# Scattering expert outputs with ScalarE and GpSimd instead of VectorE, with seven split-weight buffers and seven loaded tiles instead of five and nine

## The chip, the cores and the metric

The kernel runs on one core of a Trainium2 chip. The metric is the device time of one launch in microseconds (us). The core has five engines that each work through their own list of instructions in order and wait for each other through semaphores: TensorE (PE in the profile; its weight loads are PEld), VectorE (DVE), ScalarE (ACT), GpSimd (POOL) and SyncE (SP), which here issues the large loads from memory.

## What is computed

A trunk of two layers over 256 latent and 256 context tokens of width 1024. Each layer has a token mixer and a channel mixer. In the second layer the channel mixer is a mixture of experts, and only the latent tokens go through it:

```
def swiglu(u, w1, w3, w2):
    return (jax.nn.silu(u @ w1) * (u @ w3)) @ w2

def moe_swiglu(u, router_w, router_b, w1, w3, w2):
    logits = (u @ router_w + router_b).astype(F32)
    top_v, top_i = lax.top_k(logits, TOP_K)            # 2 of 8 experts
    gates = jax.nn.softmax(top_v, axis=-1)
    combine = jnp.sum(jax.nn.one_hot(top_i, N_EXPERTS, dtype=F32) * gates[..., None], axis=-2)
    out = jnp.zeros_like(u)
    for e in range(N_EXPERTS):                         # w1, w3: 1024 x 2816, w2: 2816 x 1024
        out = out + combine[..., e:e + 1] * swiglu(u, w1[e], w3[e], w2[e])
    return out
...
h_lat = layer_norm(ALPHA * h_lat + mod_l[5] * f_lat, ln_g, ln_b)
```

## The kernel before

All matrices are float32. A product is made of three passes of the faster fp32r type: each operand is cast to fp32r (its high part), the difference to the original is its low part, and `mm3` adds high times high, high times low and low times high (lines 107 to 109). For a weight this is the work of `split`: 1024 columns of a loaded tile are cast by ScalarE into `whi` (L126), and VectorE subtracts to get `wlo` (L127). One such pair is called a split below; six matmuls of 512 columns use it. Five pairs of buffers (the pool `wp`) hold the splits that wait for TensorE or are in use, so ScalarE can be at most five ahead.

The mixture is run in units of up to 128 tokens for one expert; `moe` has seven units written out, and a loop behind them for further ones, which does not run on this input. For each unit, `gather` picks the rows with a one-hot matmul, `turn` transposes them, `up` makes one of six chunks of 512 hidden columns (w1 and w3; the last has 256), `turn_g` transposes the result, `down` multiplies by w2 into the two accumulators `Y`, and after the sixth chunk `scatter` brings `Y` back to the rows of the tokens. Work of the next unit is interleaved with the end of one: its first `up` chunk stands ahead of the last `down`, and its second `up` chunk runs beside the scatter. Weights come as tiles of 1 MB (`wtile`), issued by SyncE in the order of use into nine buffers: seven of the pool `rawb` and two of `rawp`. A tile makes two splits and is free for the next load when VectorE has read it for the second `wlo`.

`scatter` first splits `Y` into `yh` (ScalarE) and `yl` (VectorE). For each of four quarters (two groups of 128 tokens, two halves of 512 columns) TensorE makes a one-hot matmul into a bank of the tag `T`, of which there are two; VectorE takes it out of PSUM, scaling it by the combine weight `cu` of each row and by the modulation `gate` of each column (L1131), into a tile `sct`; and GpSimd adds it to the residual stream `hl` (L1132). `sct` comes from the pool `mo`, which holds two buffers of each name. The last unit passes `quick=True` and does part of its adds on VectorE.

The order of each engine's list is fixed when the program is built, by a scheduler that sees all dependences; nothing is reordered on the chip. An instruction that waits holds up all that stand behind it on its engine.

Of the kernel before, what the change touches and what calls it, by code (L numbers as in the profile page):

```python
# [15 lines left out]
F32 = mybir.dt.float32  # L16
# [3 lines left out]
AF = mybir.ActivationFunctionType  # L20
ALU = mybir.AluOpType
# [3 lines left out]
P = 128  # L25
# [51 lines left out]
class Trunk:  # L77
# [41 lines left out]
    def split(self, v, pool=None):  # L119

        nc = self.nc
        a, b = v.shape[1], v.shape[2]
        pool = pool or self.wp
        hi = pool.tile([P, 1024], F32R, name="whi", tag="whi")[:, 0:a * b].rearrange("p (a b) -> p a b", a=a)
        lo = pool.tile([P, 1024], F32R, name="wlo", tag="wlo")[:, 0:a * b].rearrange("p (a b) -> p a b", a=a)
        nc.scalar.copy(out=hi, in_=v)  # L126
        self.last = nc.vector.tensor_tensor(out=lo, in0=v, in1=hi, op=ALU.subtract)  # L127
        return hi, lo
# [988 lines left out]
    def scatter(self, Y, selT, cu, gate, hl, quick=False):  # L1117

        nc, mp = self.nc, self.mp
        yh, yl = (mp.tile([P, D], F32R, name=name, tag="rows") for name in ("yh", "yl"))  # L1120
        for nn in range(2):
            cs = slice(nn * 512, nn * 512 + 512)
            self.split2(yh[:, cs], yl[:, cs], Y[nn])
        for b in range(2):
            for nn in range(2):
                cs = slice(nn * 512, nn * 512 + 512)
                o = self.bank("h" if quick else "T")
                nc.tensor.matmul(o, lhsT=selT[:, b], rhs=yh[:, cs], start=True, stop=False)
                nc.tensor.matmul(o, lhsT=selT[:, b], rhs=yl[:, cs], start=False, stop=True)
                t = mp.tile([P, 512], F32, name="sct", tag="g" if quick and nn else "sct")  # L1130
                nc.vector.scalar_tensor_tensor(out=t, in0=o, scalar=cu[:, b:b + 1], in1=gate[:, cs], op0=ALU.mult, op1=ALU.mult)  # L1131
                (nc.vector if quick and nn else nc.gpsimd).tensor_tensor(out=hl[:, b, cs], in0=hl[:, b, cs], in1=t, op=ALU.add)  # L1132

    def moe_consts(self, ro):

# [107 lines left out]
    def run(self):  # L1243
        tc, nc, i = self.tc, self.nc, self.i
# [4 lines left out]
        with ExitStack() as es:  # L1249
            pool = lambda name, bufs, **kw: es.enter_context(tc.tile_pool(name=name, bufs=bufs, **kw))  # L1250
            self.cp = pool("cp", 1)
            self.stp = pool("stp", 4)
            self.rawp = pool("rawp", 2)
            self.wp = pool("wp", 5)
            pool("edge", 1, side="right").tile([P, 24], F32, name="edge")
            mx = ExitStack()
            right = lambda name, bufs, **kw: mx.enter_context(tc.tile_pool(name=name, bufs=bufs, side="right", **kw))
# [31 lines left out]
            hl = pool("hl", 1).tile([P, 2, D], F32, name="hl")  # L1289
            with tc.tile_pool(name="hc", bufs=1) as hcp:  # L1290
                hc = hcp.tile([P, 2, D], F32, name="hc")
                h = lambda tb: hc[:, tb] if tb < 2 else hl[:, tb - 2]
                with tc.tile_pool(name="raw2", bufs=2) as raw2, tc.tile_pool(name="ga", bufs=1) as gp, tc.tile_pool(name="res", bufs=1) as self.resp:
                    nc.gpsimd.dma_start(out=hc, in_=i["ctx"].rearrange("o (b p) d -> p (o b) d", p=P))
                    nc.gpsimd.dma_start(out=hl, in_=i["x"].rearrange("o (b p) d -> p (o b) d", p=P))
                    gate = self.gate(0, 2, [0, 1], gp)
# [33 lines left out]
            self.moe_consts(pool("rc", 1))  # L1330
            mh, ml = self.mixer(1, uh, ul, lat, bd, self.lru_products(1, uh, ul, True), prepare)
            self.dumpm(mh, ml, 1)
            self.RB, self.wn = 7, 0
            self.rawb = pool("rawb", self.RB)
            ro = pool("ro", 1)
            gate2 = self.gate(1, 5, [0], ro)[0]
            with ExitStack() as ms:
# [54 lines left out]
```

## Time and profile before

| | |
|---|---|
| median of 3 runs | 1671.74 us (1671.57 to 1671.98) |
| the profiled execution | 1673.18 us |
| its span, first to last instruction | 1671.3 us |
| busy share of the span | PE 95%, DVE 73%, ACT 55%, POOL 10% |
| experts' part with the scatters | from about 943 to 1658 us of the span |

The span is that of the one execution that was traced; 1.9 us of its time lie outside it. A matmul's record lasts longer than the distance to the next one, since matmuls overlap in the array, so a busy share of TensorE close to 100% does not say that it runs at its peak, and gaps in its records understate a wait a little.

### The profile page before, as it was taken

Reading aid. Unit: us, or ns where it says so; the run is one execution under the profiler, and the core shown is the slowest. Engines: PE = TensorE matmul, PEld = TensorE weight load, DVE = VectorE, ACT = ScalarE, POOL = GpSimd, SP = SyncE. Lnnn points to the kernel's source line nnn. Section 1 sums busy time; section 2 is a strip of 40 time slices with the busy share of each in tenths; the row PEclk is TensorE's granted clock in tenths of the full one; section 3 lists DMA queues with packets and bytes.
Section 4 is the critical chain, followed back from the end, with each engine's and each line's share of the span. In section 5 each row is a group of like instructions: output and inputs, shape, how many; then the busy total and the mean of one; then the engine's idle time right before and its main releaser. Section 6 shows DMA issues by size and latency. Waiting matters only on the chain. (4 is left out here: it accounts for less than half of the span.)

```text
span 1671.3 us, 21565 instructions
## 1 busy us (share of the span) xinstructions
PE 1587.6 (95%) x7977; PEld 1229.7 (74%) x7977; DVE 1221.2 (73%) x1741; ACT 919.8 (55%) x1298; POOL 160.9 (10%) x131
## 2 busy tenths in 40 slices
PE   7999999999999999989899799999999999999995
PEld 3776566787777777777567588787887878878784
DVE  2678675644443345687976998989888898888987
ACT  2466565423222223246665487777776776767773
POOL 0000012250000000260002200101001010010101
PEclk8999999999999999989999799999999999999998
DMA  8313446224542354212348599898998989989890
GB/s 304 121 54 104 152 152 201 101 94 158 170 157 101 126 166 162 76 54 82 113 141 285 177 393 358 322 377 304 352 347 312 344 316 341 356 310 335 325 355 31
DMA packets 164582, 364.77 MB, mean 218 GB/s; under 512 B 8396, under 2 KB 46120, under 8 KB 159352
## 3 DMA queue, kind: packets, MB, share of 16 engines
q1 hardware_dynamic: 159472, 355.56, 60.6%
q0 software_dynamic: 1840, 6.67, 1.2%
q10 hardware_dynamic: 3160, 1.12, 0.3%
q8 instruction: 64, 1.05, 0.3%
q14 instruction: 46, 0.38, 0.1%
HBM read 362.27 MB, written 1.05 MB: 217 GB/s over the span
## 5 line engine op out<-in xcount | busy, mean ns | idle before, releaser
L127 DVE TENSOR_TENSOR wlo<-rawb,whi 128x1024 fp32r<-128x1024 f32 x362 | 436.0, 1249 | 34.5 <-ACT whi L126 30.6
L126 ACT CAST whi<-rawb 128x1024 fp32r<-128x1024 f32 x362 | 364.3, 1051 | 57.0 <-PE ps_h L109 33.6
L127 DVE TENSOR_TENSOR wlo<-raw,whi 128x1024 fp32r<-128x1024 f32 x214 | 269.2, 1279 | 100.1 <-ACT whi L126 98.7
L126 ACT CAST whi<-raw 128x1024 fp32r<-128x1024 f32 x214 | 218.7, 1051 | 183.8 <-DMA raw<-in_ffn_w_dram 85.6
L108 PE MATMUL ps_h<-wlo,th 128*128 128x512 f32 (+1 forms) x672 | 257.6, 383 | 14.2 <-DVE wlo L127 13.3
L107 PE MATMUL ps_h<-whi,th 128*128 128x512 f32 (+1 forms) x672 | 253.7, 378 | 0.2 <-ACT th L131 0.2
L109 PE MATMUL ps_h<-whi,tl 128*128 128x512 f32 (+1 forms) x672 | 251.8, 375 | 0.0
L108 PEld LDWEIGHTS ps_h<-wlo,th 128*128 128x128 f32 x672 | 127.3, 189 | 51.2 <-DVE wlo L127 30.6
L107 PEld LDWEIGHTS ps_h<-whi,th 128*128 128x128 f32 x672 | 127.5, 190 | 23.0 <-ACT th L131 0.5
L109 PEld LDWEIGHTS ps_h<-whi,tl 128*128 128x128 f32 x672 | 127.4, 190 | 20.6 <-DVE tl L132 0.2
L108 PE MATMUL ps_Y<-wlo,gTh 128*128 128x512 f32 x308 | 122.4, 397 | 0.4
L109 PE MATMUL ps_Y<-whi,gTl 128*128 128x512 f32 x308 | 120.2, 390 | 0.0
L1132 POOL TENSOR_TENSOR hl<-hl,sct 128x512 f32<-128x512 f32 x26 | 45.0, 1759 | 679.5 <-DVE sct L1131 559.5
L107 PE MATMUL ps_Y<-whi,gTh 128*128 128x512 f32 x308 | 108.4, 390 | 0.0
L107 PE MATMUL ps_acc<-uh,whi 128*128 128x512 f32 (+1 forms) x256 | 92.4, 367 | 2.6 <-ACT whi L126 2.3
L108 PE MATMUL ps_acc<-ul,whi 128*128 128x512 f32 (+1 forms) x256 | 94.1, 368 | 0.1
L109 PE MATMUL ps_acc<-uh,wlo 128*128 128x512 f32 (+1 forms) x256 | 92.1, 361 | 0.0
L108 PE MATMUL ps_S<-ul,whi 128*128 128x512 f32 (+1 forms) x240 | 85.7, 357 | 0.0
L107 PE MATMUL ps_S<-uh,whi 128*128 128x512 f32 (+1 forms) x240 | 85.6, 357 | 0.0
L109 PE MATMUL ps_S<-uh,wlo 128*128 128x512 f32 (+1 forms) x240 | 84.9, 355 | 0.0
L107 PE MATMUL ps_acc<-whi,uh 128*128 128x512 f32 (+1 forms) x176 | 71.0, 403 | 0.0
L108 PE MATMUL ps_acc<-wlo,uh 128*128 128x512 f32 (+1 forms) x176 | 69.1, 392 | 0.2 <-DVE wlo L127 0.2
(352 smaller groups left out, 2830.3 us busy)
## 6 DMA issues: line engine op xcount, KB each, us to landing
rawb<-in_moe_w_dram SPq DMA_DIRECT2D x181, 1024.0 KB, 6.7
raw<-in_moe_w_dram SPq DMA_DIRECT2D x50, 1024.0 KB, 6.5
raw<-in_ada_w_dram SPq DMA_DIRECT2D x40, 1024.0 KB, 4.9
raw<-in_ffn_w_dram SPq DMA_DIRECT2D x33, 1024.0 KB, 7.2
raw<-in_w_in_dram SPq DMA_DIRECT2D x16, 1024.0 KB, 5.6
aw<-in_ada_w_dram SPq DMA_DIRECT2D x16, 512.0 KB, 7.0
raw<-in_w_out_dram SPq DMA_DIRECT2D x16, 512.0 KB, 5.6
lg<-in_ln_g_dram POOLq DMA_DIRECT2D x4, 512.0 KB, 4.0
```

What stands on the lines that cost most here:

```text
L107: mm(out, lhsT=ah, rhs=bh, start=start, stop=False)
L108: mm(out, lhsT=ah, rhs=bl, start=False, stop=False)
L109: mm(out, lhsT=al, rhs=bh, start=False, stop=stop)
L126: nc.scalar.copy(out=hi, in_=v)
L127: self.last = nc.vector.tensor_tensor(out=lo, in0=v, in1=hi, op=ALU.subtract)
L1132: (nc.vector if quick and nn else nc.gpsimd).tensor_tensor(out=hl[:, b, cs], in0=hl[:, b, cs], in1=t, op=ALU.add)
```

## The change

Three edits. In `scatter`, for all units but the last (`quick`), the copy out of PSUM moves from VectorE to ScalarE, which scales by `cu` only; GpSimd multiplies by `gate` and then adds, two instructions where it had one. The split pairs get seven buffers from the start of the second layer's output projection on: the five of `wp` and two of a new pool `wpx`, used in turn. The pool `rawb` shrinks from seven tiles of 1 MB to five, so that seven are loaded ahead instead of nine; the memory that this frees holds `wpx`. A small tile (`shift`) moves the addresses behind it by 384 bytes per partition.

```diff
@@ split
-        pool = pool or self.wp
+        if pool is None:
+            pool = self.wps[self.ws % len(self.wps)]
+            self.ws += 1
@@ scatter
-                nc.vector.scalar_tensor_tensor(out=t, in0=o, scalar=cu[:, b:b + 1], in1=gate[:, cs], op0=ALU.mult, op1=ALU.mult)
-                (nc.vector if quick and nn else nc.gpsimd).tensor_tensor(out=hl[:, b, cs], in0=hl[:, b, cs], in1=t, op=ALU.add)
+                if quick:
+                    nc.vector.scalar_tensor_tensor(out=t, in0=o, scalar=cu[:, b:b + 1], in1=gate[:, cs], op0=ALU.mult, op1=ALU.mult)
+                    (nc.vector if nn else nc.gpsimd).tensor_tensor(out=hl[:, b, cs], in0=hl[:, b, cs], in1=t, op=ALU.add)
+                else:
+                    nc.scalar.activation(out=t, in_=o, func=AF.Copy, scale=cu[:, b:b + 1])
+                    nc.gpsimd.tensor_tensor(out=t, in0=t, in1=gate[:, cs], op=ALU.mult)
+                    nc.gpsimd.tensor_tensor(out=hl[:, b, cs], in0=hl[:, b, cs], in1=t, op=ALU.add)
@@ run
-            self.wp = pool("wp", 5)
+            self.wps, self.ws = [pool("wp", 5)] * 5, 0
...
-            self.RB, self.wn = 7, 0
+            self.RB, self.wn = 5, 0
             self.rawb = pool("rawb", self.RB)
+            pool("shift", 1).tile([P, 96], F32, name="shift")
+            self.wps, self.ws = self.wps + [pool("wpx", 2)] * 2, 0
```

The lists of the engines change with it. On ScalarE, around the scatter of the third unit (`yh` is the split of `Y`, `whi` a cast of weights, `gTh` and `g` belong to `turn_g` and `up`), this stood before:

```order
L126 CAST whi<-rawb 128x1024 x6
L131 CAST yh<-ps_Y 128x512 x2
L126 CAST whi<-rawb 128x1024 x4
L131 CAST gTh<-ps_T 128x512
L126 CAST whi<-raw 128x1024 x2
L1041 ACTIVATE g<-ps_h 128x512
L126 CAST whi<-raw 128x1024 x2
L126 CAST whi<-rawb 128x1024 x8
```

And this stands there now:

```order
L128 CAST whi<-rawb 128x1024 x4
L128 CAST whi<-raw 128x1024 x2
L133 CAST yh<-ps_Y 128x512 x2
L128 CAST whi<-raw 128x1024 x2
L1137 ACTIVATE sct<-ps_T,cu 128x512 x2
L128 CAST whi<-rawb 128x1024
L1137 ACTIVATE sct<-ps_T,cu 128x512 x2
L128 CAST whi<-rawb 128x1024
L1043 ACTIVATE g<-ps_h 128x512
L133 CAST gTh<-ps_T 128x512
L128 CAST whi<-rawb 128x1024 x8
```

The four copies stand in two pairs with one cast of weights between them; the fourth cast after `yh` has moved behind the second pair.

On VectorE, at the same scatter (`wlo` is the low part of a split, `yl` that of `Y`), before:

```order
L127 TENSOR_TENSOR wlo<-rawb,whi 128x1024 x3
L132 TENSOR_TENSOR yl<-ps_Y,yh 128x512 x2
L1131 SCALAR_TENSOR_TENSOR sct<-ps_T,cu,gate_7558 128x512 x2
L127 TENSOR_TENSOR wlo<-rawb,whi 128x1024
L1131 SCALAR_TENSOR_TENSOR sct<-ps_T,cu,gate_7558 128x512 x2
L127 TENSOR_TENSOR wlo<-rawb,whi 128x1024 x2
L132 TENSOR_TENSOR gTl<-ps_T,gTh 128x512
```

Now:

```order
L129 TENSOR_TENSOR wlo<-rawb,whi 128x1024
L129 TENSOR_TENSOR wlo<-raw,whi 128x1024 x2
L134 TENSOR_TENSOR yl<-ps_Y,yh 128x512 x2
L129 TENSOR_TENSOR wlo<-raw,whi 128x1024 x2
L129 TENSOR_TENSOR wlo<-rawb,whi 128x1024 x2
L134 TENSOR_TENSOR gTl<-ps_T,gTh 128x512
```

The four copies are gone from it, and four low parts follow `yl` directly.

## Rows read from the trace of the kernel before

**Rows 1.** The page, part 1: busy us, share of the span, instructions.
```profile
PE 1587.6 (95%) x7977; PEld 1229.7 (74%) x7977; DVE 1221.2 (73%) x1741; ACT 919.8 (55%) x1298; POOL 160.9 (10%) x131
```

**Rows 2.** Windows with a scatter: PE, PEld, DVE, ACT, POOL busy; PEclk; DMA share; GB/s.
```profile
1050.00:1100.00 50.00, 49.32 (x222) 39.86 (x222) 48.20 (x46) 38.30 (x41) 7.03 (x4) 1.00 0.91 339
...
1150.00:1200.00 50.00, 48.48 (x216) 38.85 (x216) 43.36 (x42) 35.92 (x40) 7.02 (x4) 1.00 0.88 317
...
1250.00:1300.00 50.00, 47.18 (x203) 37.59 (x202) 42.60 (x41) 33.07 (x39) 7.02 (x4) 0.97 0.90 319
...
1350.00:1400.00 50.00, 47.03 (x207) 36.92 (x206) 44.23 (x43) 32.83 (x38) 7.02 (x4) 1.00 0.92 327
...
1450.00:1500.00 50.00, 47.09 (x200) 36.90 (x199) 43.50 (x42) 34.73 (x40) 7.01 (x4) 0.97 0.88 316
...
1550.00:1600.00 50.00, 47.00 (x206) 36.70 (x205) 43.98 (x42) 32.93 (x38) 7.01 (x4) 1.00 0.92 334
```

**Rows 3.** Waits, 1040 to 1660 us: total us, times, longest.
```profile
ACT whi L126 <- PE ps_h L109: 30.3, 61, 1.7
...
PE ps_h L108 <- DVE wlo L127: 13.3, 15, 1.2
```

**Rows 4.** Timeline of the third scatter, all engines: start, us, engine, instruction [idle <-releaser].
```profile
1249.70 1.08 ACT L131 CAST yh<-ps_Y 128x512 fp32r<-128x512 f32 x2 [2.07 <-PE ps_Y L109]
...
1249.97 0.40 PE L107 MATMUL ps_h<-whi,th 128*128 128x512 f32 x1
...
1250.20 0.40 PE L108 MATMUL ps_h<-wlo,th 128*128 128x512 f32 x1
...
1250.67 3.90 ACT L126 CAST whi<-rawb 128x1024 fp32r<-128x1024 f32 x4
...
1251.07 1.28 DVE L132 TENSOR_TENSOR yl<-ps_Y,yh 128x512 fp32r<-128x512 f32 x2
...
1252.56 1.44 DVE L1131 SCALAR_TENSOR_TENSOR sct<-ps_T,cu,gate 128x512 f32<-128x512 f32 x2 [0.21 <-PE ps_T L1129]
...
1253.39 7.02 POOL L1132 TENSOR_TENSOR hl<-hl,sct 128x512 f32<-128x512 f32 x4 [94.76 <-DVE sct L1131]
...
1253.91 1.87 DVE L127 TENSOR_TENSOR wlo<-rawb,whi 128x1024 fp32r<-128x1024 f32 x1
...
1255.84 0.50 PE L108 MATMUL ps_h<-wlo,th 128*128 128x512 f32 x1 [0.83 <-DVE wlo L127]
...
1257.32 0.60 PE L1052 MATMUL ps_T<-cst,g 128*128 128x128 f32 x4
...
1257.62 3.87 DVE L127 TENSOR_TENSOR wlo<-rawb,whi 128x1024 fp32r<-128x1024 f32 x2
...
1257.67 0.48 PE L107 MATMUL ps_h<-whi,th 128*128 128x512 f32 x1
...
1259.32 0.50 PE L108 MATMUL ps_h<-wlo,th 128*128 128x512 f32 x1 [1.16 <-DVE wlo L127]
...
1261.55 0.69 PE L108 MATMUL ps_h<-wlo,th 128*128 128x512 f32 x1 [0.82 <-DVE wlo L127]
...
1262.47 0.63 PE L107 MATMUL ps_h<-whi,th 128*128 128x512 f32 x1
```

**Rows 5.** Low parts (`wlo`), 1270 to 1340 us, no GpSimd work: ns min/median/max.
```profile
L127 DVE TENSOR_TENSOR wlo<-rawb,whi x39: 1207/1219/1226, 1269.3 to 1339.0; 128x1024 fp32r<-128x1024 f32 x39
```

**Rows 6.** Tile `sct`, third scatter: ns min/median/max.
```profile
L1131 DVE SCALAR_TENSOR_TENSOR sct<-ps_T,cu,gate x4: 740/750/751, 1252.6 to 1257.0; 128x512 f32<-128x512 f32 x4
L1132 POOL TENSOR_TENSOR hl<-hl,sct x4: 1285/1780/2271, 1253.4 to 1258.1; 128x512 f32<-128x512 f32 x4
```

**Rows 7.** Tile `p` near 885 us, ScalarE from PSUM with one per-row operand: ns min/median/max.
```profile
L614 ACT ACTIVATE p<-ps_S,nb x3: 671/683/688, 880.5 to 886.2; 128x512 f32<-128x512 f32 x3
```

**Rows 8.** SyncE's own waits, 1040 to 1660 us.
```profile
SPq L1006 <- DVE wlo L127: 452.6, 179, 7.5
```

**Rows 9.** The page, part 6: KB each, us from issue to landing.
```profile
rawb<-in_moe_w_dram SPq DMA_DIRECT2D x181, 1024.0 KB, 6.7
```

## The prediction

> **What bounds the kernel now.** I read the page's busy shares first, then the windows, then the waits of the experts' part, then the timeline of one scatter. TensorE is busy 95% of the span [rows 1], so time is won or lost almost only where TensorE stands still. In the windows with a scatter it is busy 49.3, 48.5, 47.2, 47.0, 47.1 and 47.0 of 50 us [rows 2]; that is 0.68 + 1.52 + 2.82 + 2.97 + 2.91 + 3.00 = 13.9 us idle at the six scatters that the change touches. Nearly all of it is one wait: TensorE for the low part `wlo`, 13.3 us in 15 waits [rows 3]. Elsewhere ScalarE waits for TensorE (30.3 us in 61 waits [rows 3]): the five pairs of split buffers are full, and TensorE sets the pace.
>
> Records of matmuls last 0.40 us and start 0.23 us apart [rows 4], so a gap understates a wait by about 0.17 us; 15 waits make 2.4 us, and the loss at the six scatters is about 13.9 + 2.4 = 16.3 us.
>
> The timeline shows who is late. At the third scatter TensorE waits for `wlo` at 1255.84, 1259.32 and 1261.55 [rows 4]. VectorE has then spent 1.28 us on `yl`, four times 0.75 on the copies [rows 6], and its low parts have become slow: 1.87 us for one and 3.87 for two [rows 4], against 1.22 where GpSimd does nothing [rows 5]. GpSimd's adds suffer too: 1.29 us at best, 2.27 at worst [rows 6]. The numbers fit turns taken one after the other: the add of 2.27 us is one of about 1.25 that first waited for a low part, and the low part is late by the add ahead of it. The copies are not touched: 740 to 751 ns [rows 6] beside the same adds. They read PSUM and one tile of SBUF; a low part reads two tiles of SBUF, as GpSimd's add does.
>
> So I price a low part at 1.15 us (1.22 with the overlap of consecutive ones taken off), a GpSimd instruction at 1.25, and let them take turns.
>
> **The change, part by part, at one scatter.**
>
> *Removed:* four copies on VectorE, 1.44 us a pair [rows 4], 2.9 us in all. They lie on the engine that is late, so by themselves they would be worth up to 2.9 us of the 2.7 lost per scatter (16.3 / 6).
>
> *Added on ScalarE:* four copies. The nearest row reads PSUM, writes 128x512 and takes one per-row operand: 0.68 us [rows 7]. ScalarE is busy 33 to 38 of 50 us in these windows [rows 2], so the 2.7 us of work cost nothing by themselves. What costs is the wait that comes with them: `sct` has two buffers, so the third copy waits until GpSimd has multiplied and added the first quarter, and the fourth until it has done the second. In the new order one cast stands between the pairs and all further casts behind the second pair. Whatever ScalarE waits there, the splits wait.
>
> *Added on GpSimd:* four multiplications of the shape of the add, 1.25 us alone, up to 2.27 beside low parts. Nothing bounds them from below but the 1.25.
>
> *The walk*, on the third scatter's own clock [rows 4]. ScalarE ends `yh` and two casts (3.90 / 4 each) at 1252.6, makes copies 1 and 2 until 1253.9, the one cast until 1254.85, and waits. VectorE ends `yl` at 1252.35 and makes low part A until 1253.5. Then in turns: multiplication 1 to 1254.75, low part B to 1255.85, addition 1 to 1257.1. Copy 3 ends at 1257.85. Low part C to 1258.2, multiplication 2 to 1259.45, addition 2 to 1260.7. Copy 4 ends at 1261.4, and only now comes the next cast, D, done at 1262.4. VectorE has no low part to make in the meantime; multiplication and addition 3 run to 1263.2, D's low part to 1264.35. `g` and `gTh` (0.54 us each, as `yh`) stand before cast E, and each of E's and F's low parts alternates with a GpSimd instruction: 1266.75 and 1269.1.
>
> TensorE starts the next chunk at 1249.97. Four splits (24 matmuls) and the eight scatter matmuls at 0.2275 us take it to 1257.25. The four transposes of `g` need the bank that copy 3 empties: 0.65 us of wait, then 0.4 of work (1257.32 to 1257.67 [rows 4]). The fifth split lasts to 1259.7; the sixth is D, whose cast ends at 1262.4: 2.75 us. D's low part costs another 1.7, E's 0.97 and F's 1.0, since a turn of 2.4 us stands against 1.365 us that TensorE takes for a split. Together 7.1 us.
>
> *Sum.* Six scatters at 7.1 make 42.6 us. At the first two TensorE loses 2.2 and 1.4 us less than the later 2.9 today [rows 2], because it reaches them with more splits in hand; I give the new ones the same 3.6 us back. 42.6 - 3.6 - 16.3 = 22.7 us more than before. The seventh scatter is `quick` and unchanged.
>
> *Two more split buffers.* They hold what ScalarE is ahead. With the order above it is not the buffers but the wait for GpSimd that stops it, so nothing is taken off; at most they give two splits, 2.7 us a scatter, if TensorE arrives with both filled (a rival below). Below nothing: no instruction is added, and a pair that is free earlier makes nobody wait.
>
> *Seven loaded megabytes.* Nine hold 18 splits, 24.6 us of TensorE's work; seven hold 14, 19.1 us. A load lands 6.7 us after its issue [rows 9], and SyncE waits 452.6 us for VectorE to free a tile [rows 8], so loads are issued as soon as there is room and lie ready long before they are cast. Cost nothing, hidden by 12 us of cover; if that were gone, each late load would stop TensorE by what it is late. The 384 bytes by which tiles move: nothing in these rows depends on an address.
>
> The sum is on differences inside the traced execution (1673.18 us, a span of 1671.3 and 1.9 outside it), which lies 1.4 us above the median of the runs, 1671.74. On the median: 1671.7 + 22.7 = 1694.4, say 1695.
>
> **A rule against the row.** The rows show VectorE late at each scatter and ScalarE with a quarter of its time free. The Trainium skill, Perfetto Trace Analysis, § Optimizing Scalar/DVE Operations, says that work may go from a saturated VectorE to ScalarE or even GpSimd, and warns in the same paragraph that VectorE and GpSimd share a port, so that moving work between them might not help. By its first half the 16.3 us would shrink; by the rows, GpSimd's instructions double and each holds up a low part. The trace agrees with the warning (1.87 us against 1.22).
>
> **The rivals.**
>
> *The relief works (faster).* If low parts stayed at 1.22 us beside GpSimd, addition 1 would end at 1255.9 and addition 2 at 1258.5, cast D at 1260.2 and its low part at 1261.3; TensorE, at 1259.05, would lose 1.15 + 0.9 = 2.05 us, six times 12.3 against 16.3: 4 us less, 1668. With all waits gone it would be 1655. For it: the 2.9 us less on VectorE. Against it: 1.87 and 2.27. It decides where GpSimd's eight instructions take under 11 us instead of some 15. The rule's first half is this rival. Chance 8%.
>
> *The buffers carry it (slower by less).* TensorE arrives with two more splits: 7.1 - 2.7 = 4.4 us a scatter, 26.4 - 3.6 - 16.3 = 6.5 us: 1678. For it: ScalarE waits for full buffers today. Against it: D stands behind copy 4 however many buffers are free. Chance 16%.
>
> *The clock falls as well (slower by more).* After TensorE has stood still three times within 6 us at the third scatter, a matmul's record is 0.63 us instead of 0.40 [rows 4]: the lower of its two levels, 1.2 instead of 2.4 GHz. The granted clock is 0.97 in two of the six windows [rows 2], which is 0.03 x 50 = 1.5 us of full speed lost in each. With twice the standstill it may come at all six: four more, 6 us, 1701, and longer ones to 1712. Chance 20%.
>
> *Loads come late*, 1715 and more: 2%. *No difference*, the wait only changing its name: 4%, if the new chain is 4 us shorter than I walk it at every scatter.
>
> **How the numbers follow.** The forecast has 50%, at 1695. Slower by over 0.2% (3.3 us, about what a measurement of this kernel can tell from no change) are the forecast, the two rivals on its side and late loads: 50 + 16 + 20 + 2 = 88%; same 4%; faster 8%. The range goes from 1676, just under the second rival, to 1712, the long half-speed stretches, which leaves out the faster and equal cases and the late loads, 14%. The forecast's own is 1686 to 1701, a wait of 1.5 us more or less a scatter.
>
> **What would show it.** In the new profile: ScalarE's third and fourth copies idle 2 to 3 us each, ended by GpSimd's addition; eight GpSimd instructions in some 14 to 16 us at each scatter, low parts of 1.9 to 2.3 us beside them, and a gap of VectorE that ends with a cast; TensorE waiting first for a `whi` of ScalarE, then for three low parts, 7 us in all; no wait of ScalarE for a load. The prediction is wrong if the copies do not wait, if low parts beside multiplications stay at 1.2 us, or if TensorE is idle under 3 us at a scatter.

## The result and the profile after

The changed kernel takes 1694.95 us (median of 4 runs, 1693.94 to 1696.38), the one before 1671.65 on the same chip, and the ratio estimated from the executions is 1.0134 (the medians alone give 1.0139), with a 95% interval of 1.0122 to 1.0146. That is 23.3 us more by the medians and 22.4 by the ratio, where 22.7 were forecast. The profiled execution takes 1694.94 us, with a span of 1693.2.

The page's busy shares, as [rows 1] (the lines of `split` have moved down by two, so L126 and L127 are L128 and L129 from here on):

```profile
PE 1597.7 (94%) x7977; PEld 1233.8 (73%) x7977; DVE 1215.7 (72%) x1717; ACT 923.8 (55%) x1322; POOL 201.4 (12%) x155
```

The work has moved as the diff says: 24 instructions fewer on VectorE, 24 more on ScalarE and on GpSimd. None of these three engines is near its limit, and TensorE's share is hardly lower; its records have grown by 10 us. Why is in the windows of the six scatters, with the columns of [rows 2]:

```profile
1050.00:1100.00 50.00, 47.50 (x211) 37.89 (x210) 40.41 (x37) 35.29 (x42) 13.54 (x8) 1.00 0.86 307
...
1150.00:1200.00 50.00, 45.71 (x193) 35.53 (x192) 42.78 (x37) 31.80 (x38) 13.82 (x8) 0.97 0.85 308
...
1250.00:1300.00 50.00, 45.70 (x186) 35.30 (x185) 39.70 (x34) 32.95 (x39) 13.81 (x8) 0.93 0.86 305
...
1350.00:1400.00 50.00, 45.67 (x191) 35.18 (x191) 42.02 (x37) 33.03 (x40) 13.82 (x8) 0.97 0.84 302
...
1450.00:1500.00 50.00, 45.80 (x211) 36.58 (x210) 41.99 (x37) 32.50 (x39) 13.82 (x8) 0.97 0.86 308
...
1550.00:1600.00 50.00, 45.80 (x214) 36.87 (x213) 42.07 (x37) 35.71 (x43) 13.83 (x8) 0.94 0.88 314
```

TensorE is idle 2.50 + 4.29 + 4.30 + 4.33 + 4.20 + 4.20 = 23.8 us there, against 13.9 before [rows 2]. The granted clock fell in five of the six: 0.03 + 0.07 + 0.03 + 0.03 + 0.06 = 0.22, times 50 us is 11.0 us of full speed, against 3.0 before. The 8 us more stand against the 6 that one rival had put for a clock that falls at all six. Together the 9.9 us of standing still and the 8.0 of full speed make 17.9 of the 21.9 us by which the span has grown; these rows do not show where the other 4 lie. The waits, to be held against [rows 3]:

```profile
DVE wlo L129 <- ACT whi L128: 69.6, 56, 5.4
...
ACT sct L1137 <- POOL hl L1139: 26.5, 11, 2.9
...
PE ps_h L107 <- ACT whi L128: 12.3, 5, 2.5
...
PE ps_h L108 <- DVE wlo L129: 8.1, 6, 1.5
...
PE ps_T L1054 <- ACT sct L1137: 0.8, 1, 0.8
...
ACT whi L128 <- PE ps_h L109: 0.6, 2, 0.3
```

The second row is the new wait: ScalarE for GpSimd's addition, 11 times, up to 2.9 us. It is passed on: VectorE waits for ScalarE's casts, and TensorE waits for a `whi` five times, 2.5 us each, which the list of before has not once. The last row was 30.3 us before [rows 3]: ScalarE hardly ever finds the buffers full. Most of that comes with the seven pairs and not with the scatter, for run 1 below, which changes the buffers alone, has 4.8 us there. Nor has ScalarE ceased to be ahead elsewhere: it waits 68.0 and 47.8 us for TensorE at `gTh` and `g` (47.7 and 47.0 before). Of ScalarE waiting for a load there is no row.

The timeline of the third scatter shows the chain (start, length, instruction, and idle time before it); it answers to [rows 4]:

```profile
1262.30 1.39 ACT L1137 ACTIVATE sct<-ps_T,cu 128x512 f32<-128x512 f32 x2
1263.59 1.04 ACT L128 CAST whi<-rawb 128x1024 fp32r<-128x1024 f32 x1
1266.63 0.69 ACT L1137 ACTIVATE sct<-ps_T,cu 128x512 f32<-128x512 f32 x1 [2.00 <-POOL hl L1139]
1270.21 0.69 ACT L1137 ACTIVATE sct<-ps_T,cu 128x512 f32<-128x512 f32 x1 [2.89 <-POOL hl L1139]
1270.80 1.03 ACT L128 CAST whi<-rawb 128x1024 fp32r<-128x1024 f32 x1
...
1263.07 1.30 POOL L1138 TENSOR_TENSOR sct<-sct,gate 128x512 f32<-128x512 f32 x1 [92.47 <-ACT sct L1137]
1264.45 2.15 POOL L1139 TENSOR_TENSOR hl<-hl,sct 128x512 f32<-128x512 f32 x1
1266.56 2.26 POOL L1138 TENSOR_TENSOR sct<-sct,gate 128x512 f32<-128x512 f32 x1
1268.91 1.27 POOL L1139 TENSOR_TENSOR hl<-hl,sct 128x512 f32<-128x512 f32 x1
...
1275.05 2.15 POOL L1139 TENSOR_TENSOR hl<-hl,sct 128x512 f32<-128x512 f32 x1
...
1265.37 2.31 DVE L129 TENSOR_TENSOR wlo<-rawb,whi 128x1024 fp32r<-128x1024 f32 x1
1271.87 1.96 DVE L129 TENSOR_TENSOR wlo<-rawb,whi 128x1024 fp32r<-128x1024 f32 x1 [4.18 <-ACT whi L128]
...
1271.89 0.49 PE L107 MATMUL ps_h<-whi,th 128*128 128x512 f32 x1 [2.47 <-ACT whi L128]
1273.88 0.80 PE L108 MATMUL ps_h<-wlo,th 128*128 128x512 f32 x1 [1.50 <-DVE wlo L129]
1274.48 0.63 PE L109 MATMUL ps_h<-whi,tl 128*128 128x512 f32 x1
1274.90 0.63 PE L107 MATMUL ps_h<-whi,th 128*128 128x512 f32 x1
```

Read it by what each bracket names. The first addition ends at 1266.60, and copy 3 starts at 1266.63; the second ends at 1270.18, and copy 4 starts at 1270.21. Behind copy 4 stands the fourth cast (1270.80), and on that TensorE and VectorE stop, 2.47 and 4.18 us. GpSimd's instructions take either 1.27 to 1.30 us or 2.15 to 2.26; the longer ones began while VectorE was in a low part, and the low part between them takes 2.31. After the two waits TensorE's records are 0.63 us long and start 0.43 apart: the lower of its two levels.

### The profile page after: what moved, and what is told of

Its sections match the earlier page's. It is cut to its first block, busy times and chain, and to the rows that moved or that the text cites. A ratio compares the mean times of both kernels' runs of the same rounds, so it can differ in the third digit from the quotient of the medians.

```text
span 1693.2 us, 21515 instructions
## 1 busy us (share of the span) xinstructions
PE 1597.7 (94%) x7977; PEld 1233.8 (73%) x7977; DVE 1215.7 (72%) x1717; ACT 923.8 (55%) x1322; POOL 201.4 (12%) x155
## 5 line engine op out<-in xcount | busy, mean ns | idle before, releaser
L129 DVE TENSOR_TENSOR wlo<-rawb,whi 128x1024 fp32r<-128x1024 f32 x330 | 404.2, 1273 | 47.7 <-ACT whi L128 46.8
L129 DVE TENSOR_TENSOR wlo<-raw,whi 128x1024 fp32r<-128x1024 f32 x246 | 312.4, 1295 | 118.5 <-ACT whi L128 118.0
L128 ACT CAST whi<-raw 128x1024 fp32r<-128x1024 f32 x246 | 248.9, 1051 | 175.7 <-DMA raw<-in_ffn_w_dram 84.2
L128 ACT CAST whi<-rawb 128x1024 fp32r<-128x1024 f32 x330 | 326.2, 1051 | 20.3 <-PE ps_h L109 9.6
L108 PE MATMUL ps_h<-wlo,th 128*128 128x512 f32 (+1 forms) x672 | 261.4, 389 | 9.5 <-DVE wlo L129 8.4
L1138 POOL TENSOR_TENSOR sct<-sct,gate 128x512 f32<-128x512 f32 x24 | 42.3, 1762 | 580.1 <-ACT sct L1137 580.1
L107 PE MATMUL ps_T<-whi,gh 128*128 128x512 f32 x164 | 66.9, 408 | 3.4 <-DVE acc L903 3.2
```

The costliest lines, as they stand in the source:

```text
L107: mm(out, lhsT=ah, rhs=bh, start=start, stop=False)
L108: mm(out, lhsT=ah, rhs=bl, start=False, stop=False)
L1138: nc.gpsimd.tensor_tensor(out=t, in0=t, in1=gate[:, cs], op=ALU.mult)
```

## The experiments

Eleven kernels, in three groups (1 to 4, 5 to 8, 9 to 11) that each shared the runs of the kernel before on a chip of its own; its medians there are 1673.51, 1673.22 and 1672.24 us. Differences are the ratio's, on 1671.65 us. Differences of medians are within 1 us of these but for runs 1, 2 and 3, where they are 4.5, 16.5 and 12.0.

| run | time, us | ratio to before, 95% | us against before |
|---|---|---|---|
| the whole change | 1694.95 | 1.0134 (1.0122 to 1.0146) | +22.4 |
| 1 only the buffers | 1678.03 | 1.0038 (1.0023 to 1.0052) | +6.4 |
| 2 only the scatter | 1689.98 | 1.0111 (1.0094 to 1.0128) | +18.6 |
| 3 three `sct` | 1685.52 | 1.0086 (1.0070 to 1.0103) | +14.4 |
| 4 no multiplication | 1668.08 | 0.9969 (0.9960 to 0.9979) | -5.2 |
| 5 seven loaded tiles | 1677.21 | 1.0027 (1.0018 to 1.0037) | +4.5 |
| 6 three `sct`, one input | 1673.38 | 1.0001 (0.9991 to 1.0010) | +0.2 |
| 7 the wait filled | 1692.19 | 1.0115 (1.0098 to 1.0132) | +19.2 |
| 8 accumulated | 1665.87 | 0.9957 (0.9940 to 0.9974) | -7.2 |
| 9 two `sct`, one input | 1692.76 | 1.0123 (1.0106 to 1.0140) | +20.6 |
| 10 accumulated, spread | 1665.32 | 0.9961 (0.9946 to 0.9975) | -6.5 |
| 11 gate on Y | 1663.47 | 0.9948 (0.9932 to 0.9965) | -8.7 |

**1 and 2. The change in two halves.** Run 1 has the diff's hunks in `split` and `run`, run 2 the hunk in `scatter`.

> Only the buffers of the change: seven pairs of split buffers and seven loaded tiles; the scatter stays as before. The forecast's account (the time is lost by ScalarE's wait for GpSimd) expects no loss here: between 1660 us, if the two further splits cover the 2.7 us that TensorE loses at each scatter, and 1672. If the trade of loaded tiles for split buffers were what costs (loads late), 1680 or more, with waits of ScalarE for a load.

> Only the scatter of the change, with five pairs of split buffers and nine loaded tiles as before. The forecast's account took nothing off for the two further buffers, so it expects the time of the whole change, 1692 to 1700 us, with the same waits of the third and fourth copy. If the buffers carry part of the wait, as one rival had it, up to 2.7 us more is lost at each of six scatters without them: 1700 to 1711. If the trade of buffers were what costs, this kernel would be back at 1672 to 1680.

Both fell outside. Two windows of run 2, the first and the third scatter:

```profile
1050.00:1100.00 50.00, 47.16 (x209) 37.49 (x209) 43.11 (x39) 37.68 (x42) 13.63 (x8) 1.00 0.86 319
...
1250.00:1300.00 50.00, 46.03 (x192) 35.76 (x191) 42.02 (x38) 32.66 (x39) 13.81 (x8) 0.93 0.83 296
```

The third stands almost as in the whole change (45.70), with five pairs of split buffers instead of seven. The buffers cost 6.4 us (3.8 to 8.7), which the forecast had put at nothing, and the scatter by itself 18.6 (15.7 to 21.4), which the forecast had put at 22.7. Added up, the halves make 25.0 us by the ratios and 21.0 by the medians, against 22.4 and 23.3 for the whole: the forecast of 22.7 was met because the two misses have opposite signs. Two things were not so: that the buffers carry part of the wait (run 2 would be slower than the whole), and that their trade is all that costs.

**5. Which buffers.** The kernel before, with one number changed:

```
-            self.RB, self.wn = 7, 0
+            self.RB, self.wn = 5, 0
```

> The kernel before with seven loaded tiles instead of nine and nothing else (five pairs of split buffers). Changing the buffers alone had cost some 5 us, and this tells which half of the trade it is. If the two missing loaded tiles cost it (through the order of the lists, which is planned with them: at the second scatter ScalarE's list then has one cast less ahead of yh, as in the kernel with all of the trade): 1675 to 1680 us, with the second scatter losing as much as the third. If the two further split buffers cost it: 1670 to 1674, as before.

1677.21 us: the two loaded tiles alone cost 4.5 us (3.0 to 6.2), so the split buffers add nothing that can be told. The windows of the first three scatters of this run, as [rows 2]:

```profile
1050.00:1100.00 50.00, 49.40 (x222) 39.76 (x221) 45.76 (x44) 36.97 (x41) 7.01 (x4) 1.00 0.90 330
...
1150.00:1200.00 50.00, 47.03 (x207) 36.93 (x206) 44.25 (x43) 32.56 (x38) 7.02 (x4) 1.00 0.90 327
...
1250.00:1300.00 50.00, 47.01 (x205) 36.66 (x204) 45.56 (x44) 33.18 (x37) 7.01 (x4) 1.00 0.90 328
```

The second scatter, which lost 1.5 us before, loses 3.0 like all later ones. That is 1.5 of the 4.5 us. It isn't that loads come late: the list of waits has none of ScalarE for a load, and a tile still lands 6.6 us after its issue, as [rows 9]. The timeline of ScalarE at this scatter shows other waits instead:

```profile
1148.19 1.99 ACT L126 CAST whi<-rawb 128x1024 fp32r<-128x1024 f32 x2
1152.26 1.08 ACT L131 CAST yh<-ps_Y 128x512 fp32r<-128x512 f32 x2 [2.08 <-PE ps_Y L109]
1153.22 3.90 ACT L126 CAST whi<-rawb 128x1024 fp32r<-128x1024 f32 x4
1160.52 0.59 ACT L131 CAST gTh<-ps_T 128x512 fp32r<-128x512 f32 x1 [3.40 <-PE ps_T L1052]
```

ScalarE stands 2.08 and 3.40 us behind instructions that need TensorE, with casts behind them in its list. The program's order differs from before at this place, though not a line of the scatter has changed. ScalarE's list ahead of the second `yh` and behind it, before:

```
L131 CAST gTh<-ps_T 128x256
L126 CAST whi<-rawb 128x1024 x2
L126 CAST whi<-raw 128x1024 x3
L131 CAST yh<-ps_Y 128x512 x2
L126 CAST whi<-raw 128x1024
L126 CAST whi<-rawb 128x1024 x4
L1041 ACTIVATE g<-ps_h 128x512
L131 CAST gTh<-ps_T 128x512
```

and with seven loaded tiles:

```
L126 CAST whi<-raw 128x1024 x4
L126 CAST whi<-rawb 128x1024 x2
L131 CAST yh<-ps_Y 128x512 x2
L126 CAST whi<-rawb 128x1024 x4
L131 CAST gTh<-ps_T 128x512
L126 CAST whi<-rawb 128x1024 x2
L1041 ACTIVATE g<-ps_h 128x512
```

Five casts stood between `yh` and the next instruction that waits for TensorE, now four. The scheduler plans with the loads that it expects, and writes another list. That this list is the cause is argued from the waits; loads and list could not be changed one without the other. Nor is the whole cost at this scatter. From the first `yh` to the third run 5 takes 203.5 us (1052.25 to 1255.80), the kernel before 200.5 (1049.20 to 1249.70): 3.0 us, of which 1.3 lie in the unit behind the first scatter, at its end, where the lists differ too. From the third `yh` on the traced run 5 is no slower, and where the rest of the 4.5 us lies is not shown.

**3. ScalarE's wait taken away in part.** Three buffers of `sct` in the changed kernel:

```
-                t = mp.tile([P, 512], F32, name="sct", tag="g" if quick and nn else "sct")
+                t = mp.tile([P, 512], F32, name="sct", tag="g" if quick and nn else "sct", bufs=2 if quick and nn else 3)
```

> The changed kernel with three buffers of sct for ScalarE's copies instead of two; the order of every engine's list is the same. GpSimd still runs its eight instructions. The third copy then finds a free buffer and the fourth waits for the first addition only, some 3.5 us earlier than for the second. If ScalarE's wait is the cause, the fourth cast comes about that much earlier and 3 to 4 us of the 7 lost per scatter go: 1671 to 1680 us. If the cause is only that eight GpSimd instructions take turns with the low parts, nothing goes: 1690 to 1696.

1685.52 us lies between the two. The wait for GpSimd fell from 26.5 us to 7.3, and TensorE no longer waits for any `whi`; but it now waits for low parts 33 times, about 0.55 us each:

```profile
PE ps_Y L108 <- DVE wlo L129: 9.1, 18, 0.6
PE ps_h L108 <- DVE wlo L129: 8.7, 15, 0.6
ACT sct L1137 <- POOL hl L1139: 7.3, 5, 1.5
```

So both causes are there, and the second stands behind the first.

**9 and 6. The turns taken away.** GpSimd multiplies by a constant instead of the tile `gate`, so it reads one tile of SBUF instead of two, and the gating is left out. The lists keep their order. Run 9 has two buffers of `sct`, run 6 three.

```
-                    nc.gpsimd.tensor_tensor(out=t, in0=t, in1=gate[:, cs], op=ALU.mult)
+                    nc.gpsimd.tensor_scalar(out=t, in0=t, scalar1=1.0, scalar2=None, op0=ALU.mult)
```

> The changed kernel with its two buffers of sct, and GpSimd's multiplication by a constant instead of the gate (the gating is left out); the order of every list is that of the changed kernel. With three buffers the same edit took 12 us off (1685.5 to 1673.4). If the wait of ScalarE and the turns simply add up, it takes as much off here: 1681 to 1685 us. If the wait for GpSimd is long enough to cover the turns of multiplications, which then only lengthen or shorten that wait, it takes off less, some 0.75 us at each of the two quarters that the fourth copy waits for: 1685 to 1690.

> Three buffers of sct, and GpSimd's multiplication takes a constant instead of the gate (the gating is left out), so that it reads one tile of SBUF instead of two; the order of every list is that of the kernel with three buffers. If what is left there is turns between two-input instructions of GpSimd and VectorE, four of the eight turns of a scatter go, 0.75 us each at TensorE: some 2 to 3 us at six scatters, 1667 to 1675 us. If any instruction of GpSimd holds up the low parts, whatever it reads: 1683 to 1688.

With three buffers the edit takes off 12 us by the medians (14 by the ratios) and brings the time back to that of before. With two it takes off 2 us, which is not told from nothing (20.6 against 22.4, with intervals that overlap), and less than either expectation: ScalarE waits as long as ever, and a multiplication by a constant is no shorter (1.49 us with VectorE idle, in the second row, against 1.26 in the changed kernel).

```profile
ACT sct L1137 <- POOL hl L1139: 26.9, 12, 3.1
```
```profile
1268.64 1.49 POOL L1138 TENSOR_SCALAR sct<-sct 128x512 f32<-128x512 f32 x1
```

That VectorE is held up less shows in the groups of the experts' part (count, busy us, mean ns, idle before). Run 3:

```profile
L1139 POOL TENSOR_TENSOR hl<-hl,sct 128x512 f32<-128x512 f32 x24 | 50.9, 2120 | 1.9
```
```profile
L129 DVE TENSOR_TENSOR wlo<-rawb,whi 128x1024 fp32r<-128x1024 f32 x279 | 355.3, 1323 | 32.1 <-ACT whi L128 31.7
```

Run 6:

```profile
L1138 POOL TENSOR_SCALAR sct<-sct 128x512 f32<-128x512 f32 x24 | 53.1, 2214 | 561.3 <-ACT sct L1137 561.3
```
```profile
L1139 POOL TENSOR_TENSOR hl<-hl,sct 128x512 f32<-128x512 f32 x24 | 32.8, 1365 | 2.0
```
```profile
L129 DVE TENSOR_TENSOR wlo<-rawb,whi 128x1024 fp32r<-128x1024 f32 x279 | 343.3, 1280 | 32.5 <-ACT whi L128 31.8
```

The low parts of `rawb` alone are 12 us shorter in all, and GpSimd's additions stand 1.37 us instead of 2.12. The multiplications do not gain: 2.21 us in the mean, 2.02 in run 3. They still wait for low parts; it is the low parts that wait less for them.

**4. Less work on GpSimd.** The changed kernel without the line `nc.gpsimd.tensor_tensor(out=t, in0=t, in1=gate[:, cs], op=ALU.mult)`.

> The changed kernel without GpSimd's multiplication by the gate (the gating is left out); the lists of the other engines keep their order and sct its two buffers. A quarter then holds its buffer for one GpSimd instruction instead of two, so the fourth copy can start 2.5 to 4 us earlier, and three fewer low parts have to take turns. Both accounts, the wait and the turns, expect most of the loss gone: 1660 to 1672 us. If what costs is the copies on ScalarE by themselves, it stays above 1685.

1668.08 us, 5.2 less than before. The copies on ScalarE are no burden by themselves: each still takes 0.69 us, and VectorE is relieved as the rival "the relief works" had it, once GpSimd does no more than before. That the kernel is then faster shows what the change would have brought with a free gate.

**7. The clock.** Where TensorE waits for the fourth cast and its low part, ten and six matmuls with a tile of zeros:

```
+                        for _ in range(10 if at else 0):
+                            nc.tensor.matmul(b, lhsT=self.zero, rhs=fill[0][:, 1], start=False, stop=False)
...
+                            for _ in range(6):
+                                nc.tensor.matmul(b, lhsT=self.zero, rhs=wh[:, kk], start=False, stop=False)
```

> The changed kernel with matmuls that add zero where TensorE waits: ten ahead of the first matmul with the fourth cast and six ahead of the one with its low part (0.2275 us each: 2.3 and 1.4 us of waits of 2.6 and 1.8). The lists of ScalarE, VectorE and GpSimd keep their order at the scatters. TensorE then hardly stands still before the next two low parts, and its clock should stay at the higher level. If the lower clock only fills the time until those low parts come, they are waited for instead, about 1 us each, and the time stays at 1692 to 1698 us. If the lower clock costs time of its own, the 8 us of full speed that the changed kernel loses more than the one before come back: 1685 to 1689.

1692.19 us, 3.2 less than the change by the ratios, at the lower edge of the first expectation and far from the second. The third scatter's window, and the waits for low parts (the last row is that of the filled place):

```profile
1250.00:1300.00 50.00, 48.21 (x209) 37.59 (x208) 42.26 (x38) 36.81 (x43) 13.91 (x8) 1.00 0.85 311
```
```profile
PE ps_h L108 <- DVE wlo L129: 7.7, 14, 0.6
...
PE ps_h L1044 <- DVE wlo L129: 0.8, 5, 0.2
```

The granted clock is 1.00 in all six windows, so all 11.0 us of full speed are back, and 3.2 us are seen in the time, by ratios whose intervals overlap: TensorE gets through its next matmuls sooner and waits for the low parts behind them, 14 times. The traces tell more closely what the lower clock cost. From `yh` to the first matmul of the next `down` both kernels have the same work but for the zeros. The changed kernel takes 20.2 us for it at the three scatters whose window has 0.97, and 21.2 at the two with 0.93 and 0.94; run 7 takes 20.2 to 20.3 at all five. So the lower clock cost 1 us at two scatters and nothing at three: it mostly fills a wait that would be there anyway. (Further on the lists of the two kernels differ, and what else their times differ by is not told from the clock.) Where no late low part follows, it has its price: the kernel before takes 18.8 us for the same stretch at the third and fifth scatter (0.97) and 17.6 at the fourth and sixth (1.00).

**8, 10 and 11. Other ways to relieve the scatter.** All three from the kernel before, 8 and 10 with eight loaded tiles. In run 8 VectorE adds the scaled rows into a tile `acc`, and GpSimd multiplies that by the gate and adds it to `hl` once, behind the sixth scatter; in run 10 VectorE does this closing work, in four pieces during the last unit; in run 11 VectorE multiplies `Y` by the gate first and adds straight to `hl`.

```
+    nc.vector.scalar_tensor_tensor(out=acc[:, b, cs], in0=o, scalar=cu[:, b:b + 1], in1=acc[:, b, cs], op0=ALU.mult, op1=ALU.add)
```
```
+    nc.vector.tensor_tensor(out=t, in0=Y[nn], in1=gate[:, cs], op=ALU.mult)
+    self.split2(yh[:, cs], yl[:, cs], t)
...
+    nc.vector.scalar_tensor_tensor(out=hl[:, b, cs], in0=o, scalar=cu[:, b:b + 1], in1=hl[:, b, cs], op0=ALU.mult, op1=ALU.add)
```

> Another way to take load off the scatter, from the kernel before: VectorE adds the scaled rows out of PSUM into a tile of its own, one instruction per quarter, and GpSimd multiplies that by the gate and adds it to hl once, after the sixth scatter. Eight loaded tiles instead of nine make room. GpSimd does nothing at the first five scatters. If the turns with GpSimd make VectorE late, its low parts stay at 1.2 us there and 1.5 to 2.5 us per scatter go: 1658 to 1667 us. If VectorE is late by its own copies, the time stays: 1669 to 1675.

> The kernel that accumulates, with the eight closing instructions (times gate, added to hl) on VectorE and spread over the last unit, one pair to each of four chunks, instead of on GpSimd directly behind the sixth scatter. There TensorE lost 4.0 us of 50 in the window of the sixth scatter, and 0.4 in that of the fifth. If those 3 to 4 us were turns with GpSimd and VectorE has room in mid-unit: 1661 to 1664 us, faster than both kernels. If VectorE has no room there: 1666 to 1668.

> From the kernel before, with nine loaded tiles: VectorE multiplies Y by the gate ahead of its split (two instructions of 128x512 more), and one instruction per quarter scales the rows out of PSUM and adds them to hl; GpSimd does nothing at the six scatters. Without the turns some 1.5 to 2.5 us a scatter go, and the two multiplications of 0.7 us bring 1.4 back, with yh waiting for them: 1662 to 1670 us. If the longer chain from Y to yh stops TensorE: 1672 or more.

Runs 8 and 11 came as expected, and run 11 is the fastest kernel here: 1663.47 us, 0.52% (0.35 to 0.68) below the kernel before, though the intervals of runs 8 and 10 overlap with its own. The fifth and sixth scatter of run 8, without and with GpSimd at work, in windows:

```profile
1450.00:1500.00 50.00, 49.59 (x219) 39.31 (x219) 43.56 (x44) 34.78 (x41) 0.00 (x0) 1.00 0.96 341
...
1550.00:1600.00 50.00, 45.98 (x192) 34.95 (x192) 47.19 (x41) 32.17 (x36) 15.60 (x8) 0.97 0.84 298
```

VectorE makes its four copies at both (a quarter's instruction takes as long as before), and TensorE is idle 0.4 us at the one and 4.0 at the other. It is GpSimd's turns that made VectorE late at the scatters before, not the copies. Run 10 came out between its two expectations. Its sixth window comes to 48.60, but three of the four pieces stop TensorE 1.0 us each, the first of them at the end of this window and the others later in the unit, so no gain on run 8 can be told (-6.5 against -7.2 us): VectorE has little room there. In run 11 the low parts around the third scatter stay at 1.2 us and the instructions on PSUM at 0.75, with no GpSimd beside them (ns, min/median/max):

```profile
L127 DVE TENSOR_TENSOR wlo<-rawb,whi x5: 1215/1216/1220, 1248.6 to 1257.8; 128x1024 fp32r<-128x1024 f32 x5
```
```profile
L1140 DVE SCALAR_TENSOR_TENSOR hl<-ps_T,cu,hl x4: 742/748/751, 1251.1 to 1254.2; 128x512 f32<-128x512 f32 x4
```

## Why the prediction was right, and where it wasn't

*The chain of waits held, step by step.* ScalarE's third and fourth copies wait 2.00 and 2.89 us for GpSimd's addition (2 to 3 forecast), a copy takes 0.69 us (0.68), the eight GpSimd instructions take 14.1 us at the third scatter (1263.07 to 1277.20; 14 to 16), low parts beside them 2.31 (1.9 to 2.3). TensorE waits 2.47 us for the `whi` and 1.50 for its low part; with the 0.17 us by which a gap understates a wait, 2.64 and 1.67 (2.75 and 1.7). On the walk's clock, with the 9.73 us taken off by which this `yh` starts later, copy 4 starts at 1260.48 (1260.7) and D's low part is done at 1264.10 (1264.35). Runs 3, 6 and 9 show that this is the cause and in which order: the wait for GpSimd comes first (with it, the turns hardly matter, run 9), the turns second (with the wait cut down, taking the gate out of four of the eight instructions gives back 12 to 14 us, run 3 against run 6, and the time is that of before).

*The bank of `T`* was sized at 0.65 us a scatter and is seen as a wait of a matmul once in six. At the third scatter the first transpose starts 0.50 us behind the matmul ahead of it, where 0.23 is the distance: 0.27 us.

*The last two waits* (0.97 and 1.0 us) are not in the trace as waits. TensorE came to those low parts at half speed and found them ready. The rival "the clock falls as well" was right about the clock and wrong about its price: it was to come on top, 6 us and more, and run 7 shows that it takes the place of these two waits and costs some 2 us besides.

*The credit of 3.6 us* for the first two scatters is about what run 2 shows for the scatter alone: its windows are idle 2.84 and 2.73 us there against 3.97, 4.34, 4.34 and 4.19 later, 2.9 us less in all, and the granted clock is 1.00 in these two and 0.93 to 0.97 in the others. In the whole change only the first is better (2.50; the second 4.29).

*The scatter's own term*, sized at 22.7 us, measured 18.6 in run 2, and what was mis-sized is what it was held against: the 16.3 us of the kernel before. The chunk beside a scatter is 56 matmuls and four transposes, 13.1 us by the prediction's prices. From its first matmul to the first of the next `down` the changed kernel takes 19.9 to 21.0 us at the third to sixth scatter. That is 6.8 to 7.9 lost, with 7.1 forecast. The kernel before takes 17.3 or 18.5: 4.2 or 5.4 lost, where the prediction had 2.9 idle and 0.5 for gaps that understate. It left out the lower clock, 1.2 us at two of the scatters, and 0.8 us that no row of its waits names. (And 15 times 0.17 is 2.6, not 2.4, which would have moved the forecast by 0.2.)

*"Cost nothing", for the seven loaded tiles, is the step that failed*: 4.5 us by run 5. The cover of the loads was argued from their landing [rows 8, 9], and that holds; what was not weighed is that the lists of all engines are planned anew when the number of tiles changes. The rows for it lay open in the lists of the two kernels, where the second scatter could have been compared as the third was. Against this stands the scatter's own term. So that the total was met within 1 us is luck: two misses of about 4 us cancel, inside the range in either case.

*Two more split buffers: nothing taken off.* Right as far as can be told (runs 1 and 5 do not differ: 6.4 and 4.5 us, with intervals that overlap), and nothing speaks against the reason given, that the casts stand behind waits in the list.

*The relief* had its condition named rightly: it decides where GpSimd's part is short. Run 4, with four GpSimd instructions in about 8 us of a scatter, is 5.2 us faster than before; with eight in 14 us the change is on the other side. That it lands on the 1668 us of that rival is chance: the rival had eight instructions without turns, and not the cost of the loaded tiles. *The buffers carry it* (1678) is out by run 2, which is not slower without them.

## What to carry to other kernels

Before moving an instruction to an idle engine, look at what it must wait for there and at what stands behind it in that engine's list: here 2.8 us of copies fitted easily into ScalarE's free time, but two of them waited for GpSimd, and every later cast with them. A pair of engines that take turns on two-tile instructions is relieved by taking work off the pair, not by moving it within it; run 11 does the same sum with GpSimd idle and is faster than both kernels. And where a scheduler writes the order, a buffer count is an edit of the order: compare the lists at each place where a term of the sum lies, not at one.

## What the runs showed of the hardware that was not expected

The GpSimd instruction that reads one tile of SBUF held up VectorE less than the one that reads two. They are different instructions too (TENSOR_SCALAR and TENSOR_TENSOR), so that the number of tiles makes the difference is not shown. In run 6, first VectorE, then GpSimd, around the third scatter:

```profile
1256.30 2.76 DVE L129 TENSOR_TENSOR wlo<-raw,whi 128x1024 fp32r<-128x1024 f32 x2
1258.98 2.33 DVE L129 TENSOR_TENSOR wlo<-rawb,whi 128x1024 fp32r<-128x1024 f32 x1
```
```profile
1257.37 1.49 POOL L1138 TENSOR_SCALAR sct<-sct 128x512 f32<-128x512 f32 x1 [88.20 <-ACT sct L1137]
1258.94 1.29 POOL L1139 TENSOR_TENSOR hl<-hl,sct 128x512 f32<-128x512 f32 x1
1260.20 2.47 POOL L1138 TENSOR_SCALAR sct<-sct 128x512 f32<-128x512 f32 x1
```

The low part that meets the start of an addition takes 2.33 us, 1.1 more than the 1.22 of [rows 5]; the second of the pair at 1256.30, which meets the start of a multiplication by a constant, takes about 1.6 (2.76 less the 1.13 to the start of the second), 0.4 more. The multiplication itself is held up by a low part, by 1.0 us: 2.47 against 1.49. The Trainium skill, SBUF — State Buffer, § Who interferes with whom, says that a VectorE instruction with two inputs in SBUF contends with a GpSimd instruction that reads SBUF, and that ScalarE never waits for another engine's use of SBUF; the traces agree with both (low parts of 2.31 us beside additions in the changed kernel, ScalarE's copies at 0.69 there).

And the lower clock cost at most 1 us a scatter in the changed kernel, after stops of 2.5 and 1.5 us and with late low parts behind it (run 7), but 1.2 us in the kernel before, where no late low part followed.
